# Row sums of a 67 MB tensor: splitting the first load by 64 bytes per partition in place of one row

## The chip, the cores and the metric

The kernel runs on one core of one Trainium2 chip. The metric is device time in microseconds (us) of that core, as the median of several executions. Spans and event times come from one profiled execution, counted from its first instruction; a span is some 1.8 us shorter than the time of the same execution.

## The reference

The input has 32 x 512 rows of 1024 float32 values, and each row is summed.

```python
def setup_inputs():
    return {"x": np.random.randn(32, 512, 1024).astype(np.float32)}

def reference(x):
    return np.sum(x, axis=-1).astype(np.float32)
```

So 67.1 MB are read and 65 KB are written, and there is one addition per value.

## The kernel before

Partition p of a block reads `n` whole rows that follow one another in memory. Three buffers of 16 rows per partition (8 MB each) take turns; a load of buffer k+3 waits for the reduction of buffer k. The first buffer alone is filled by two loads. The first `EARLY` instructions of the issuing engine (SP), which are these two loads, are moved ahead of the start barrier.

```python
BLOCKS = (112, 16)
G = 16
EARLY = 2
...
    xpool = ctx.enter_context(tc.tile_pool(name="x", bufs=3))
...
        while c < whole:
            m = min(G, whole - c)
            xt = xpool.tile([P, G * D], F32, tag="xt", name="xt")
            parts = (0, 1, m) if done + c == 0 else (0, m)
            for i, k in zip(parts, parts[1:]):
                nc.sync.dma_start(
                    out=xt[:, i * D : k * D], in_=x_b[:, (c + i) * D : (c + k) * D]
                )
            a = ACT_ROWS if done + c + m == full else 0
            rows_dve(xt, res, 0, m - a, c)
            rows_act(xt, res, m - a, a, c + m - a)
            c += m
# ... the last 16 rows are loaded in five smaller pieces and summed on VectorE and ScalarE ...
    loads = [i for i in code if i.engine == sp][:EARLY]
# ... these loads are taken out of the body and put ahead of the start barrier ...
```

## Time and profile before

| | before |
|---|---|
| time, median of 3 (range) | 162.22 us (162.12 to 162.32) |
| span of the profiled execution | 160.6 us |
| full-width reduction, and the load it waits for | 17.22 us, every 19.35 us |
| one packet of 65536 bytes on one DMA engine | 2418 ns |
| last data landed | 157.8 us |

These are lines of the profile page of the kernel before: the span; VectorE's (DVE) busy time; the busy share of the DMA engines in 40 slices, in tenths; the chain of work that ended last; the costliest group; and the larger of the first two loads, with its size and the time from issue to landing.

```profile
span 160.6 us, 119 instructions
...
DVE 121.5 (76%) x16; ACT 17.2 (11%) x31; POOL 0.2 (0%) x4
...
DMA  9988996996996996996996996996996996998991
...
DMA 75%; DVE 23%; SPq 0%; issue 0%; DVEq 0%
...
L43 DVE TENSOR_REDUCE res<-xt 128x16 f32<-128x16384 f32 (+3 forms) x9 | 119.8, 13309 | 36.5 <-DMA xt<-in_x_dram 36.5
...
xt<-in_x_dram SPq DMA_DIRECT2D x1, 7680.0 KB, 21.5
...
```

DVE is busy for three quarters of the span, yet it isn't the limit, as its timeline shows. The columns are start, duration (both us), engine (in these views ACT is ScalarE and POOL is GpSimd), line, operation, operands, and in brackets the idle time before it with what ended that.

```profile
...
22.00 17.22 DVE L43 TENSOR_REDUCE res<-xt 128x16 f32<-128x16384 f32 x1 [22.00 <-DMA xt<-in_x_dram]
...
60.63 17.22 DVE L43 TENSOR_REDUCE res<-xt 128x16 f32<-128x16384 f32 x1 [2.13 <-DMA xt<-in_x_dram]
...
118.67 17.22 DVE L43 TENSOR_REDUCE res<-xt 128x16 f32<-128x16384 f32 x1 [2.13 <-DMA xt<-in_x_dram]
138.03 9.75 DVE L43 TENSOR_REDUCE res<-xt 128x9 f32<-128x9216 f32 x1 [2.13 <-DMA xt<-in_x_dram]
...
158.21 0.08 DVE L59 DVE_READ_ACCUMULATOR2_ANT res<- 128x1 f32 x1
```

The full-width reductions take 17.22 us, and from the third on each one starts only after a wait of 2.13 us for a DMA. Consecutive ones start 19.35 us apart (118.67 less 60.63, over three). The loads set the pace.

The records of single DMA packets, which the page sums up, give the pace of a load. One packet is one partition's contiguous run, and each of the 16 DMA engines takes eight of them per load, one after the other (the records don't name the engine; I read this from starts that follow ends). A packet of 65536 bytes takes 2418 ns and one of 4096 bytes 159 ns, so the rate is (65536 - 4096) / (2418 - 159) = 27.2 bytes per ns with some 8 ns per packet on top. Sixteen engines make 435 GB/s of it. The Trainium skill, "DMA: Bandwidth & Descriptors", section Specifications, gives 435 GB/s as the fabric ceiling; this trace agrees. Later loads are issued about 20 us before an engine gets to them (one was issued at 39.24 us and its first packet started at 59.50 us), so from its first packet on no engine is short of work.

That makes the start worth a look. The following lines are stretches of the first 6 us of the kernel before. After the stretch and its length come the busy times of the compute engines, then the clock, the busy share of the DMA engines, and GB/s.

```profile
...
core 0: us, DVE busy (x) ACT busy (x) POOL busy (x), PEclk, DMA share, GB/s
0.00:0.90 0.90, 0.00 (x0) 0.00 (x0) 0.20 (x4) 1.00 0.00 0
0.90:1.45 0.55, 0.00 (x0) 0.00 (x0) 0.00 (x0) 1.00 1.15 156
1.45:2.60 1.15, 0.00 (x0) 0.00 (x0) 0.00 (x0) 1.00 0.75 267
2.60:3.45 0.85, 0.00 (x0) 0.00 (x0) 0.00 (x0) 1.00 3.05 1311
...
4.90:5.90 1.00, 0.00 (x0) 0.00 (x0) 0.00 (x0) 1.00 2.27 983
...
```

In this view a packet is booked whole in the stretch in which it starts, so a share far above 1 means long packets starting. From 2.60 to 3.45 us, 1311 GB/s over 0.85 us are 1114 KB: sixteen packets of 61440 bytes and the last 32 of the row load. From 0.90 to 2.60 us only the row load runs. At full rate its eight packets per engine need 8 x 159 ns = 1.27 us, but they last from about 1.1 to 3.0 us, because the first ones of each engine took up to 828 ns. I call this loss, packet times above the full-rate time, the *slow start*: summed and divided by 16 it comes to 0.55 us per engine here, all within the row load. The big packets behind it had none (2267 to 2274 ns).

The row load's landing, by the list of DMA issues (size and time from issue to landing; its other line is the rest of the first buffer):

```profile
...
xt<-in_x_dram SPq DMA_DIRECT2D x1, 7680.0 KB, 21.5
...
xt<-in_x_dram SPq DMA_DIRECT2D x1, 512.0 KB, 3.8
...
```

### The profile page before, as it was taken

Reading aid. Unit: us, or ns where it says so; the run is one execution under the profiler, and the core shown is the slowest. Engines: PE = TensorE matmul, PEld = TensorE weight load, DVE = VectorE, ACT = ScalarE, POOL = GpSimd, SP = SyncE. Lnnn points to the kernel's source line nnn. Section 1 sums busy time; section 2 is a strip of 40 time slices with the busy share of each in tenths; the row PEclk is TensorE's granted clock in tenths of the full one; section 3 lists DMA queues with packets and bytes.
Section 4 is the critical chain, followed back from the end, with each engine's and each line's share of the span. In section 5 each row is a group of like instructions: output and inputs, shape, how many; then the busy total and the mean of one; then the engine's idle time right before and its main releaser. Section 6 shows DMA issues by size and latency. Waiting matters only on the chain.

```text
span 160.6 us, 119 instructions
## 1 busy us (share of the span) xinstructions
DVE 121.5 (76%) x16; ACT 17.2 (11%) x31; POOL 0.2 (0%) x4
## 2 busy tenths in 40 slices
DVE  0000059997799959999499994999949998697884
ACT  0000000000000000000000000000000000695892
POOL 0000000000000000000000000000000000000000
DMA  9988996996996996996996996996996996998991
GB/s 375 490 367 367 490 522 277 506 522 277 506 522 261 522 522 261 522 522 261 522 506 277 522 506 277 522 506 277 522 506 277 522 490 294 441 431 364 436 390 44
DMA packets 2160, 67.18 MB, mean 418 GB/s; under 512 B 496, under 2 KB 624, under 8 KB 880
## 3 DMA queue, kind: packets, MB, share of 16 engines
q1 hardware_dynamic: 2016, 67.12, 97.2%
q10 hardware_dynamic: 144, 0.06, 0.1%
HBM read 67.11 MB, written 0.07 MB: 418 GB/s over the span
## 4 chain that ended last, share of the span: by engine, by line
DMA 75%; DVE 23%; SPq 0%; issue 0%; DVEq 0%
DMA xt<-in_x_dram 75%; DVE res L43 21%; DVE pairs L59 1%; SPq L95 0%; DVE seen L112 0%; DVE part L59 0%; DVE res L59 0%; DVEq L120 0%
## 5 line engine op out<-in xcount | busy, mean ns | idle before, releaser
L43 DVE TENSOR_REDUCE res<-xt 128x16 f32<-128x16384 f32 (+3 forms) x9 | 119.8, 13309 | 36.5 <-DMA xt<-in_x_dram 36.5
L51 ACT ACT_TABLE_LOAD x1 | 1.3, 1283 | 138.1 <-DMA xt<-in_x_dram 138.1
L51 ACT ACTIVATE xt<-xt 128x1024 f32<-128x1024 f32 x15 | 15.6, 1044 | 2.4 <-DMA xt<-in_x_dram 2.3
L51 ACT ACTIVATION_READ_ACCUMULATOR xt<-xt 128x1 f32 x15 | 2.8, 187 | 0.0
L59 DVE CUSTOM_DVE_ANT_0 pairs<-xt 128x512 f32<-128x512 f32 (+1 forms) x2 | 1.1, 567 | 0.2 <-DMA xt<-in_x_dram 0.2
L59 DVE CUSTOM_DVE_ANT_0 pairs<-xt,part 128x240 f32<-128x240 f32 x1 | 0.5, 468 | 0.0
L112 DVE COPY seen<-part 128x1 f32<-128x1 f32 x1 | 0.2, 153 | 0.0
L59 DVE DVE_READ_ACCUMULATOR2_ANT res<- 128x1 f32 x2 | 0.2, 83 | 0.0
L157 POOL MEMSET const-uint8-127<- 128x1 uint8 x1 | 0.1, 102 | 0.0
L157 POOL MEMSET const-bfloat16-1.0<- 128x1 bf16 x1 | 0.1, 101 | 0.0
L157 POOL MEMSET const-float32-0.0<- 128x1 f32 x1 | 0.1, 99 | 0.2 <-issue 0.2
L157 POOL MEMSET const-float32-1.0<- 128x1 f32 x1 | 0.1, 99 | 0.0
L59 DVE DVE_READ_ACCUMULATOR2_ANT part<- 128x1 f32 x1 | 0.1, 83 | 0.0
## 6 DMA issues: line engine op xcount, KB each, us to landing
xt<-in_x_dram SPq DMA_DIRECT2D x1, 7680.0 KB, 21.5
xt<-in_x_dram SPq DMA_DIRECT2D x1, 4608.0 KB, 32.5
xt<-in_x_dram SPq DMA_DIRECT2D x1, 2048.0 KB, 37.1
xt<-in_x_dram SPq DMA_DIRECT2D x1, 1024.0 KB, 39.1
xt<-in_x_dram SPq DMA_DIRECT2D x1, 512.0 KB, 3.8
xt<-in_x_dram SPq DMA_DIRECT2D x1, 272.0 KB, 39.3
xt<-in_x_dram SPq DMA_DIRECT2D x1, 240.0 KB, 39.4
xt<-in_x_dram SPq DMA_DIRECT2D x6, 40.8
```

What stands on the lines that cost most here:

```text
L43: nc.vector.tensor_reduce(out=res[:, c : c + n], in_=xt[:, j * D : (j + n) * D].rearrange("p (j d) -> p j d", d=D), axis=X, op=ADD,)
L51: nc.scalar.activation(out=v, in_=v, func=COPY, accum_out=acc)
L59: nc.vector.tensor_tensor_reduce(out=pairs[:, 0 : h - a], in0=xt[:, a:h], in1=xt[:, h:b], scale=1.0, scalar=first, op0=ADD, op1=ADD, accum ...
L112: nc.vector.tensor_copy(out=seen, in_=part)
L157: nc = _bacc.Bacc("TRN2", target_bir_lowering=False, num_devices=1)
```

## The change

The intent: the first load need only be there to get the engines going, so make it as small as can be (64 bytes per partition, 8 KB in all) and leave everything else to one bulk load of 65472 bytes per partition, hoping that the tiny packets take the slow first accesses on themselves.

```diff
-            parts = (0, 1, m) if done + c == 0 else (0, m)
+            parts = (0, 16, m * D) if done + c == 0 else (0, m * D)
             for i, k in zip(parts, parts[1:]):
                 nc.sync.dma_start(
-                    out=xt[:, i * D : k * D], in_=x_b[:, (c + i) * D : (c + k) * D]
+                    out=xt[:, i:k], in_=x_b[:, c * D + i : c * D + k]
                 )
```

The order of instructions on each engine stays the same; only the shapes of the first two loads on SP differ.

## The prediction

> **What bounds the kernel now.** The input DMA. In the chain of waits the DMA of xt holds 75% of the 160.6 us span and DVE 23%, but DVE isn't the limit: each 128x16384 reduction takes 17.22 us and then waits 2.13 us for its load (timeline); loads complete every 19.35 us. In the DMA records each of 16 engines takes its packets back to back, 2418 ns for 65536 bytes, 159 ns for 4096: 27.2 bytes/ns plus about 8 ns a packet. Sixteen give 434 GB/s; the Trainium skill, "DMA: Bandwidth & Descriptors", Specifications, gives a fabric ceiling of 435 GB/s, and the trace agrees. Engines run without idle time from the first packet (1.00 us) to the last data (157.47 us); later loads are issued some 20 us before their turn. So only the start of each engine's stream and the tail can move the time, and the diff leaves the tail alone.
>
> **The start of before.** Issue of the row load begins at 0.00 us (0.376 us long), of the fifteen rows at 0.43 us. First packets start at 1.00 to 1.27 us. Eight packets of 4096 bytes per engine need 1.27 us at full rate but end at 2.70 to 3.42 us: the first two or so take 240 to 830 ns in place of 159. The 61440-byte packets follow without a gap. Counting back at full rate (19.41 us) from the end of the first buffer (20.82 to 21.54 us), each engine behaves as if it had started, without loss, at 1.41 to 2.13 us. The last engine carries its 0.7 us lag to the end and decides the time.
>
> **What the change does.** In the comparison of instruction orders only the first two SP loads differ; counts of loads and packets, semaphores, waits, DVE and ACT work stay. Each engine gets eight packets of 64 bytes and eight of 65472. Full-rate time is unchanged, by an estimate from the rates above: 8 x (11 + 2415) = 19.41 us. (64-byte packets of the final store took up to 11 ns; 1920-byte packets starting at an odd multiple of 128 bytes took the 79 ns that the rate predicts, so I expect no loss from the offset.) Gained: the small packets may absorb the slow first accesses. Lost: they run out at once, and the bulk can't flow before its own descriptors arrive, 0.43 us after the first load's, at 1.43 to 1.70 us, plus what it still meets of the first-read latency (0.1 to 0.65 us above full rate). Effective start: 1.5 to 2.3 us against 1.4 to 2.1. I expect a wash with a slight loss, +0.1 us, all on the critical path, since the stream has no slack. The same section of the skill puts line rate at 512 bytes and up; 128 tiny packets are too few to matter.
>
> **Prediction.** 162.3 us, 161.95 to 162.75 with 8 in 10. Faster by over 2%: 0.005; within 2%: 0.985; slower: 0.01.
>
> **What would show it.** The small load landing at 2 to 2.5 us instead of 3.8; first 65472-byte packets starting at 1.5 to 2.2 us, 2415 ns each; first buffer ending at 20.8 to 21.7 us; then every event shifted by one constant, with unchanged 2.13 us DVE waits and unchanged tail.
>
> **What would make it wrong.** The 64-byte offset lowering the bulk rate (5% would cost about 1 us, still within 2%); small packets served one after another at a full read latency each (8 x 0.24 us: +0.3 us or more); or the slow start being due to the volume moved in it, so that small packets even out the engines and the last one gains 0.3 us.

## The result, and the profile after

| | before | after |
|---|---|---|
| time, median of 6 runs each (range) | 162.27 us (162.12 to 162.49) | 162.81 us (162.76 to 162.90) |
| ratio after / before, 95% interval | | 1.0034 (1.0021 to 1.0047) |
| span of the profiled execution | 160.6 us | 161.0 us |

The change is 0.5 us slower. By a margin of 2% that is "the same", but the difference is clear of the noise, and it lies outside the range that I gave.

The same lines of the profile page of the kernel after:

```profile
span 161.0 us, 119 instructions
...
DVE 121.5 (75%) x16; ACT 17.2 (11%) x31; POOL 0.2 (0%) x4
...
DMA  7999999999999999999999999999989989998991
...
DMA 75%; DVE 22%; SPq 0%; issue 0%; DVEq 0%
...
L43 DVE TENSOR_REDUCE res<-xt 128x16 f32<-128x16384 f32 (+3 forms) x9 | 119.8, 13309 | 36.9 <-DMA xt<-in_x_dram 36.9
...
xt<-in_x_dram SPq DMA_DIRECT2D x1, 8184.0 KB, 22.0
...
```

The work is the same; the first slice of the DMA row fell from 9 tenths to 7. That digit does not measure the loss: in this row too a packet counts whole where it starts, and the first slice of one_load, an experiment below that runs in the time of before, is 7 as well. DVE's timeline of the kernel after:

```profile
...
22.52 17.22 DVE L43 TENSOR_REDUCE res<-xt 128x16 f32<-128x16384 f32 x1 [22.52 <-DMA xt<-in_x_dram]
...
61.13 17.22 DVE L43 TENSOR_REDUCE res<-xt 128x16 f32<-128x16384 f32 x1 [2.13 <-DMA xt<-in_x_dram]
...
119.17 17.22 DVE L43 TENSOR_REDUCE res<-xt 128x16 f32<-128x16384 f32 x1 [2.13 <-DMA xt<-in_x_dram]
138.53 9.76 DVE L43 TENSOR_REDUCE res<-xt 128x9 f32<-128x9216 f32 x1 [2.13 <-DMA xt<-in_x_dram]
...
158.60 0.08 DVE L59 DVE_READ_ACCUMULATOR2_ANT res<- 128x1 f32 x1
```

The first reduction starts 0.52 us later, and the later full-width ones stay 0.50 us late with the same waits of 2.13 us: a constant shift, as expected from a stream without slack. In the tail 0.1 us of it is gone in this pair of profiles (158.60 against 158.21). The two profiled executions took 162.43 and 162.82 us, 0.39 apart, while the medians are 0.54 apart: the profiled one of the kernel before was a little slow, so nothing is to be read into that 0.1.

The start of the kernel after, in the same stretches:

```profile
...
core 0: us, DVE busy (x) ACT busy (x) POOL busy (x), PEclk, DMA share, GB/s
0.00:0.90 0.90, 0.00 (x0) 0.00 (x0) 0.20 (x4) 1.00 0.00 0
0.90:1.45 0.55, 0.00 (x0) 0.00 (x0) 0.00 (x0) 1.00 0.16 15
1.45:2.60 1.15, 0.00 (x0) 0.00 (x0) 0.00 (x0) 1.00 2.70 911
2.60:3.45 0.85, 0.00 (x0) 0.00 (x0) 0.00 (x0) 1.00 0.00 0
...
4.00:4.90 0.90, 0.00 (x0) 0.00 (x0) 0.00 (x0) 1.00 2.19 946
4.90:5.90 1.00, 0.00 (x0) 0.00 (x0) 0.00 (x0) 1.00 0.45 196
...
```

The 1048 KB booked from 1.45 to 2.60 us (911 GB/s times 1.15 us) are exactly 16 packets of 65472 bytes: each engine's first bulk packet starts in this stretch, at 1.49 to 2.33 us by the packet records. The tiny packets before it had ended by 1.47 us, at 8 to 11 ns each: they show no slow start at all. And the second bulk packets start only from 4.58 us on, for the first ones took up to 3424 ns, not 2415. So the engines had next to nothing to do until the bulk came, and then the bulk had its slow start in full: 0.72 us per engine on average.

The list of DMA issues of the kernel after, for the two loads:

```profile
...
xt<-in_x_dram SPq DMA_DIRECT2D x1, 8184.0 KB, 22.0
...
xt<-in_x_dram SPq DMA_DIRECT2D x1, 8.0 KB, 1.8
...
```

The tiny load has landed 1.8 us after its issue, and nothing waits for it that early.

### The profile page after: what moved, and what is told of

Read it like the earlier page. It is cut to its first block, busy times and chain, and to the rows that moved or that the text cites. A ratio compares the mean times of both kernels' runs of the same rounds, so it can differ in the third digit from the quotient of the medians.

```text
span 161.0 us, 119 instructions
## 1 busy us (share of the span) xinstructions
DVE 121.5 (75%) x16; ACT 17.2 (11%) x31; POOL 0.2 (0%) x4
## 4 chain that ended last, share of the span: by engine, by line
DMA 75%; DVE 22%; SPq 0%; issue 0%; DVEq 0%
DMA xt<-in_x_dram 75%; DVE res L43 21%; DVE pairs L59 1%; SPq L95 0%; DVE seen L112 0%; DVE part L59 0%; DVE res L59 0%; DVEq L120 0%
```

## The experiments

Theory D: the first useful bytes come later by the interval between the issues of the two loads, 0.43 us, since the tiny load runs out before the bulk's packets can start. (0.43 us lie between the starts of the two issuing instructions. Between their ends it is 0.47 us, and that is the better measure: where its engines were free, a load's first packet started 0.60 to 0.66 us after the end of its issuing instruction, in every run.) The slow start is a cost of getting bulk bytes going, and a tiny load doesn't take it over. Rivals: the offset of 64 bytes or the odd size slows the bulk (O); tiny packets are costly by themselves (S); the slow start is a period after the launch that passes by itself (C, for cold; W is a variant, a warming by the row). Three more bear on what the slow start is: far addresses (P), the issue of further loads (G), or any start from rest (R).

Diffs are against the kernel after. Each kernel was timed in the same rounds as the kernel before, whose median was 162.32 us beside one_load, bulk_first, two_tiny and after_e1, and 162.22 us beside the others. All of these kernels gave correct results. The table collects the packet records; "bulk" means the packets of over 60000 bytes that fill the first buffer, slow starts are averages per engine, and the buffer's end is the end of its last packet. The packet columns are of one profiled execution each, which need not be the median one: that of one_load, at 162.59 us, was the slowest of five. The time of the profiled execution less its buffer's end is 140.67 to 140.98 us in all of these kernels but contig (141.35), so what the last engine loses at the start goes into the time whole.

```
                  first load    slow start  bulk issued  first bulk     slow start   buffer's   median us, and ratio to
run               per partition of it, us   at us        packets, mean  of bulk, us  end, us    before (same rounds)
before            4096 B        0.55        0.43         3.00           0.00         21.54      162.27
after             64 B          0.00        0.43         1.69           0.72         22.06      162.81  1.0034
one_load          none          -           0.00         1.13           0.78         21.76      162.36  1.0003
bulk_first        (64 B after)  -           0.00         1.19           0.69         21.42      162.35  1.0002
after_e1          64 B          0.00        0.77         2.00           0.63         22.35      163.06  1.0044
two_tiny          2 x 64 B      0.00        0.88         2.13           0.80         22.68      163.13  1.0052
b256              256 B         0.00        0.42         1.74           0.82         22.23      162.94  1.0040
kb1               1024 B        0.12        0.41         1.72           0.69         21.73      162.56  1.0024
kb2               2048 B        0.24        0.43         2.15           0.32         21.72      162.26  1.0003
before_e1         4096 B        0.52        0.77         2.97           0.05         21.58      162.45  1.0015
contig            none          -           0.00         1.18           0.62         21.37      162.42  1.0014
gated             none          -           0.00         1.26           0.66         21.68      162.43  1.0009
```

### One load for the first buffer (one_load)

```diff
-            parts = (0, 16, m * D) if done + c == 0 else (0, m * D)
+            parts = (0, m * D)
```

> The first buffer in one load of 128 x 65536 bytes, issued first. Theory D (the change costs the wait for the descriptors of the bulk; the slow start of about 0.6 us is paid by whatever carries the first real bytes): first bulk packets start at 1.0 to 1.3 us and take about 3.1 us, end of the first buffer 20.9 to 21.6 us, time 162.3 us, as before. Theory W (a first load of a whole row warms something up): the slow start grows, time 162.6 or more. Rivals O (the offset of 64 bytes costs) and S (tiny packets cost) also say 162.3.

Measured: 162.36 us, ratio 1.0003 (0.9990 to 1.0016). In the stretches of this kernel fifteen engines start their first big packet from 0.90 to 1.45 us (1787 GB/s over 0.55 us are 983 KB) and one just after, and the second packets start from 4.00 to 4.90 us, some 3.2 us later:

```profile
...
0.90:1.45 0.55, 0.00 (x0) 0.00 (x0) 0.00 (x0) 1.00 5.52 1787
1.45:2.60 1.15, 0.00 (x0) 0.00 (x0) 0.00 (x0) 1.00 0.14 57
...
4.00:4.90 0.90, 0.00 (x0) 0.00 (x0) 0.00 (x0) 1.00 2.69 1165
...
```

The row load of the kernel before thus bought nothing. W falls: with no row ahead of it the slow start was no worse in its effect on time. The slow start is here too, in the bulk.

### The same two loads in reversed order (bulk_first)

```diff
-            for i, k in zip(parts, parts[1:]):
+            for i, k in reversed(list(zip(parts, parts[1:]))):
```

> The two loads of the change in reversed order: 65472 bytes at offset 64 first, the 64 bytes after it. D: 162.3 us, the whole loss of 0.54 us is gone, though tiny packets and offset are still there; first 65472-byte packets start at 1.0 to 1.3 us. O or S: stays at 162.8.

Measured: 162.35 us, ratio 1.0002 (0.9989 to 1.0014). The stretches:

```profile
...
0.90:1.45 0.55, 0.00 (x0) 0.00 (x0) 0.00 (x0) 1.00 5.02 1667
1.45:2.60 1.15, 0.00 (x0) 0.00 (x0) 0.00 (x0) 1.00 0.30 114
...
4.00:4.90 0.90, 0.00 (x0) 0.00 (x0) 0.00 (x0) 1.00 2.68 1164
...
```

The same sizes, the same offset, the same tiny packets, and the whole loss is gone once the bulk is issued first. This clears O and S. The 64-byte packets, issued at 0.43 us, started only at 20.92 us, when the bulk packets of their engine were through. The Trainium skill, "DMA: Bandwidth & Descriptors", section Queues, rings and completion order, says that on each DMA engine descriptors are consumed in ring order; this run agrees. It is why the order of the two loads matters at all.

### Two tiny loads ahead of the bulk (two_tiny)

```diff
-EARLY = 2
+EARLY = 3
-            parts = (0, 16, m * D) if done + c == 0 else (0, m * D)
+            parts = (0, 16, 32, m * D) if done + c == 0 else (0, m * D)
```

> Two loads of 64 bytes before the bulk, all three issued early. D: the bulk is issued one issue interval (0.45 to 0.48 us) later than in the changed kernel, so 163.25 to 163.3 us, first bulk packets at about 1.95 us. S: about 0.5 more as well if the packets cost, but then bulk packets start late by more than the issue. O: 162.8.

Measured: 163.13 us, ratio 1.0052 (1.0039 to 1.0064). The bulk was issued 0.45 us later than in the kernel after, its first packets started 0.44 us later on average (2.13 against 1.69), and the time rose by 0.3 us in place of the 0.45 to 0.5 expected. With the width of the two intervals (0.2 us each way) that isn't clearly less than the delay. Second bulk packets now start after 4.90 us:

```profile
...
1.45:2.60 1.15, 0.00 (x0) 0.00 (x0) 0.00 (x0) 1.00 2.86 917
...
4.00:4.90 0.90, 0.00 (x0) 0.00 (x0) 0.00 (x0) 1.00 0.00 0
4.90:5.90 1.00, 0.00 (x0) 0.00 (x0) 0.00 (x0) 1.00 2.43 1047
...
```

### The bulk issued after the start barrier (after_e1)

```diff
-EARLY = 2
+EARLY = 1
```

> The changed kernel with only the 64-byte load issued early; the bulk is issued after the start barrier, at about 1.26 us instead of 0.43. D with a slow start that comes anew with each start of a bulk stream: +0.83 us over the changed kernel, 163.6 us, first bulk packets from 2.3 us still 0.6 to 0.9 us too long. If the slow start is a period after the launch that passes by itself: first bulk packets near 2.42 us long, time 162.9 to 163.1 us.

Measured: 163.06 us, ratio 1.0044 (1.0031 to 1.0056). My number for D missed, because I had taken the issue time from the kernel before: with only one load ahead of it the barrier was passed earlier, and the bulk was issued at 0.77 us, not 1.26. From 0.43 to 0.77 us are 0.34 us, and the time rose by 0.25. Measured at the end of the bulk's issuing instruction (0.855 us in the kernel after, 1.102 us here) the delay is 0.25 us too. The time alone fits what I wrote for C, but not the packets: thirteen of the sixteen first bulk packets took 2973 to 3434 ns, the slow start was 0.63 us per engine. So it did not pass by itself.

### A first load of 256 bytes (b256)

```diff
-            parts = (0, 16, m * D) if done + c == 0 else (0, m * D)
+            parts = (0, 64, m * D) if done + c == 0 else (0, m * D)
```

> The small load holds 256 bytes of each run, 2 KB per engine, 0.14 us at full rate (8 packets of about 18 ns). D: it is used up before the bulk arrives, as the 64-byte one was, so nearly the whole loss stays: 162.65 to 162.8 us. If only the 64 bytes are bad, or the slow start is paid by this load: 162.3.

Measured: 162.94 us, ratio 1.0040 (1.0027 to 1.0052), a little above what I expected. All small packets were through by 1.34 us, and the bulk's slow start was 0.82 us.

### A first load of 1024 bytes (kb1)

```diff
-            parts = (0, 16, m * D) if done + c == 0 else (0, m * D)
+            parts = (0, 256, m * D) if done + c == 0 else (0, m * D)
```

> The small load holds 1024 bytes of each run, 8 KB per engine. D: in the kernel before an engine had moved about 8 KB by 2.05 us, later than the descriptors of the bulk arrive (1.5 to 2.0 us), so no engine runs dry and the loss is gone: 162.3 us, within 0.15. If any first load smaller than a row costs: 162.6 or more.

Measured: 162.56 us, ratio 1.0024 (1.0012 to 1.0037). D's number missed. I had thought that 8 KB per engine last until 2.05 us, since they did as part of the row load. As small packets they had gone by 1.70 us, with little slow start of their own:

```profile
...
0.90:1.45 0.55, 0.00 (x0) 0.00 (x0) 0.00 (x0) 1.00 0.63 151
1.45:2.60 1.15, 0.00 (x0) 0.00 (x0) 0.00 (x0) 1.00 2.79 939
...
4.00:4.90 0.90, 0.00 (x0) 0.00 (x0) 0.00 (x0) 1.00 1.82 788
...
```

The 16 bulk packets begin in the same stretch as in the kernel after, and their slow start is nearly whole (0.69 us). Moving 8 KB per engine first fills most of the wait: by an estimate from the table the small packets are through at 1.13 + 8 x 0.046 + 0.12 = 1.62 us on average, 0.1 us before the bulk starts, where the 64-byte ones left 1.69 - (1.13 + 8 x 0.011) = 0.47 us idle. But it doesn't pay for the slow start, which is 0.12 + 0.69 = 0.81 us in the two loads together, against 0.78 in one_load. The waiting and the slow start add up, and that part of D stands; what fell is my idea of when the slow start is paid.

### A first load of 2048 bytes (kb2)

```diff
-            parts = (0, 16, m * D) if done + c == 0 else (0, m * D)
+            parts = (0, 512, m * D) if done + c == 0 else (0, m * D)
```

> The small load holds 2048 bytes of each run, 16 KB per engine (0.67 us at full rate). With 1024 bytes the small packets were through by 1.70 us and the bulk still began 0.5 us late and slow; with 4096 nothing was lost. Theory D with a slow start that belongs to bytes in bulk: the small load ends at about 2.1 to 2.4 us, after the bulk's descriptors are there, so 162.3 to 162.45 us. If each first load short of a row costs the same: 162.55 or more.

Measured: 162.26 us, ratio 1.0003 (0.9987 to 1.0019): the loss is gone. The small packets last to 2.34 us, and the slow start is shared: 0.24 us in them and 0.32 us in the bulk. With the row (4096 bytes) it lies wholly in the first load. That 2048 bytes are enough and 1024 are not rests on the timed runs alone, whose intervals overlap a little (0.9987 to 1.0019 and 1.0012 to 1.0037): the two profiled executions took 162.48 and 162.50 us, with the buffer's end at 21.72 and 21.73 us.

### The kernel before with its bulk issued after the barrier (before_e1)

```diff
-EARLY = 2
+EARLY = 1
```

> The kernel before with only the row load issued early: the bulk is issued at about 0.77 us, not 0.43. D: the row keeps the engines busy to 2.7 to 3.4 us, the descriptors of the bulk are there from about 1.7 to 2.5 us, so no change: 162.3 us; 61440-byte packets of 2267 ns without a slow start. If a later bulk issue costs by itself, as it did behind 64 bytes: 162.6.

(This diff alone is against the kernel before.) Measured: 162.45 us, ratio 1.0015 (0.9996 to 1.0035), with one run of six at 163.33 us that widens the interval. The bulk was issued at 0.77 us, as in after_e1, but behind a row it didn't matter: its first packets started at 2.75 to 3.21 us, straight after the row packets, and the buffer ended at 21.58 us. The timing alone doesn't settle it, with an interval that reaches from nothing to 0.6 us; the packet records do: no engine waited for its bulk, and the bulk's slow start was 0.05 us.

### The first buffer's data contiguous in memory (contig)

```diff
-BLOCKS = (112, 16)
+BLOCKS = (16, 96, 16)
-            parts = (0, 16, m * D) if done + c == 0 else (0, m * D)
+            parts = (0, m * D)
```

> One load for the first buffer, and the row blocks as 16, 96, 16 so that its 8 MB are contiguous in memory and not 128 runs at a distance of 448 KB. Theory P (the slow start of about 0.7 us comes from the many far addresses touched at once): first packets near 2418 ns, 161.7 us. Theory R (it is what starting an idle stream costs, wherever the data lies): first packets 3.0 to 3.6 us as in the run with one load, 162.3 us, the extra 8 KB store costing under 0.1.

Measured: 162.42 us, ratio 1.0014 (1.0001 to 1.0026). The first packets took 2651 to 3286 ns, a slow start of 0.62 us against 0.78 with one load of runs 448 KB apart. P falls as the main cause; a small share can't be excluded. The time is no test of it here: the first buffer ended at 21.37 us, 0.39 us before that of one_load, but the next reductions started up to 19.47 us apart, not about 19.35 as in one_load, and of the lead at the first reduction (0.39 us) 0.04 us was left at the fifth.

### No other loads issued meanwhile (gated)

```diff
-EARLY = 2
+EARLY = 1
+            if done + c == G:
+                nc.gpsimd.memset(xt[:, 0:4096], 0.0)
-            parts = (0, 16, m * D) if done + c == 0 else (0, m * D)
+            parts = (0, m * D)
```

> One load for the first buffer; the second load first waits for a fill of 128x4096 elements on GpSimd, some microseconds, so that no further loads are issued while the first packets run. Theory G (issuing the next loads slows the first packets): first packets near 2418 ns, 161.7 us. Theory R: first packets 3.0 to 3.6 us as before, 162.3 us, since the second load still comes long before the first is done.

Measured: 162.43 us, ratio 1.0009 (0.9996 to 1.0023). The second load was issued at 4.32 us, after every engine's first packet had been under way for over 2 us, and those first packets took 2453 to 3549 ns all the same. G falls.

### One buffer, so that every load starts from rest (one_buf)

```diff
-    xpool = ctx.enter_context(tc.tile_pool(name="x", bufs=3))
+    xpool = ctx.enter_context(tc.tile_pool(name="x", bufs=1))
-EARLY = 2
+EARLY = 1
-            parts = (0, 16, m * D) if done + c == 0 else (0, m * D)
+            parts = (0, m * D)
```

> One buffer, so that each of the seven big loads is issued only when the reduction before it is through and every stream starts from rest: a slow kernel on purpose, about 270 us. Theory R (a cost of every start from rest): the first packet of each engine in every one of these loads takes 3.0 to 3.6 us. Theory C (something that is cold only at launch): 3.0 to 3.6 us in the first load and near 2.42 us in the later ones.

Measured: 293.9 us in its single run (state unknown, which matters little for a look at packets). My 270 was too low: I had left out the last 16 rows, whose loads were issued only from 266.87 us on and took the span to 292.1 us. The stretches around the second load, which was issued at 39.21 us:

```profile
...
39.20:40.10 0.90, 0.00 (x0) 0.00 (x0) 0.00 (x0) 1.00 0.00 0
40.10:40.60 0.50, 0.00 (x0) 0.00 (x0) 0.00 (x0) 1.00 6.37 2097
40.60:43.00 2.40, 0.00 (x0) 0.00 (x0) 0.00 (x0) 1.00 0.00 0
43.00:44.20 1.20, 0.00 (x0) 0.00 (x0) 0.00 (x0) 1.00 2.02 874
44.20:45.30 1.10, 0.00 (x0) 0.00 (x0) 0.00 (x0) 1.00 0.00 0
45.30:46.70 1.40, 0.00 (x0) 0.00 (x0) 0.00 (x0) 1.00 1.73 749
...
```

2097 GB/s over 0.50 us, 874 over 1.20 and 749 over 1.40 are 1049 KB each time, 16 packets of 65536 bytes. The first 16 start about 40.3 us, the second 16 some 3.2 us later, the third 2.4 us after those. By the packet records the slow start of the seven loads was 0.76, 0.78, 0.86, 0.78, 0.74, 0.70 and 0.55 us per engine. So R holds and C falls: each start of the stream from rest pays it on average, at launch or 235 us later.

## Why the prediction was wrong

**Right.** The DMA bound and the missing slack: the whole shift of the first buffer went through every later load (0.52, then 0.50 us). The count of instructions and waits stayed, and the packets behind the first kept their rate (2415 to 2422 ns for 106 of 112, the longest 2622), with no loss from the offset of 64 bytes. I also had the sign and the mechanism of the loss: "Lost: they run out at once, and the bulk can't flow before its own descriptors arrive, 0.43 us after the first load's". Issue first and the loss goes (bulk_first); issue later still and it grows (after_e1, two_tiny).

**Wrong.** The failed step is the term set against that loss: "Gained: the small packets may absorb the slow first accesses." They absorbed nothing. Their packets took 8 to 11 ns, and the bulk behind them lost 0.72 us per engine, as much as a bulk with nothing ahead of it (0.78 in one_load). I had counted on the gain to cancel all but 0.1 of the 0.43 us; with the gain at zero the loss stands whole, and 0.54 us was measured. In the sum of the prediction this is the term "what it still meets of the first-read latency (0.1 to 0.65 us above full rate)": it measured 0.72 us on average, and up to 1.01 us in a single first packet. The other term was a little short as well: the bulk was to flow "at 1.43 to 1.70 us", and its first packets started at 1.49 to 2.33 us, 1.69 on average. The table above has the sum: mean start of the bulk plus its slow start was 1.69 + 0.72 = 2.41 us after, and 1.13 + 0.78 = 1.91 us in one_load, which runs in the time of before: 0.5 us apart, all of it from the later start.

So the "effective start" came out wrong: "1.5 to 2.3 us against 1.4 to 2.1" should have been 2.08 to 2.65 (the ends of the engines' work on the first buffer, 21.49 to 22.06 us, less 19.41). The last engine decides, and it went from 2.13 to 2.65 us. Two observations of the prediction fell with it: "2415 ns each" for the first bulk packets (they took 2422 to 3424) and "first buffer ending at 20.8 to 21.7 us" (21.49 to 22.06). The small load landed at 1.8 us, earlier than "2 to 2.5", which fits with its having met no slow accesses. The starting times of the first bulk packets (1.5 to 2.2 us predicted, 1.49 to 2.33 found) were nearly right.

Of my listed ways to be wrong none was it. The rate did not fall; the small packets were not served at a latency each; they did not even out the engines.

What stays open is what the slow start is. The runs show when it is paid: at each start of the stream from rest, by packets of 1024 bytes and up (little by those of 1024), and not by 64 or 256 bytes per packet. It isn't a fixed price of each engine's own start: in the kernels and loads with a slow start of the bulk, thirteen first packets began over 0.75 us after the first one of their load, and they lost 0 to 0.34 us, where the averages are 0.32 to 0.86. In the kernel after, the engine that came last (at 2.33 us) took 2422 ns. This suggests that it belongs to the stretch in which the engines start together. The runs rule out the launch (one_buf), the issue of further loads (gated) and mostly the distance of the addresses (contig). They don't show the mechanism. All loads here were issued by SP one after another; whether a bulk load issued at the same time by another engine would be spared the wait was not tried.

No kernel here beats that of before. One load for the first buffer equals it (1.0003) and is the simplest; a row first, or half a row (kb2), is as good.

## What to carry to other kernels

When DMA is the bound and its stream never runs dry, the time moves with the first moment at which the last engine has bulk work: put the bulk first, and don't let a small load precede it in the same queue unless it holds enough bytes to bridge the interval to the next issue (here 2048 bytes per partition did, while 1024 still cost 0.3 us by the timed runs). Don't expect a tiny load to pay a start-up cost for a large one; look at the packets of the tiny one, and if they show no such cost they haven't paid it. A row-sized first load that looks tuned may do nothing, so try without it before tuning its size.

## What the Trainium skill lacked or had wrong

- "DMA: Bandwidth & Descriptors" has no slow start of a load stream from rest. Here a load of 65536 bytes per partition lost 0.55 to 0.86 us per engine on its first packets, at every one of seven starts (one_buf); loads of 64 or 256 bytes per partition showed none, and a load of 4096 bytes held all of it (0.55 us).
- The same page, section Issuing engines are not separate DMA queues, calls the issue time of a DMA "usually small relative to the DMA itself". That is so for a load of 20 us, but when the load ahead in the queue holds 8 KB in all, one issue interval of 0.43 us (0.47 from end to end) was most of the whole effect of 0.54 us.
- The same page, section Latency and other measured facts, gives about 0.6 us to the first byte for a DMA issued from SP. The traces agree only if one counts from the end of the issuing instruction: it began at 0.00 us and took 0.38, and the first packet started at 0.99 us in the kernel after. Counted so, it was 0.60 to 0.66 us in every run here. From the start of the issue it is 1.0 us, and the mean over the engines is 1.1 (one_load); the page doesn't say which is meant.
- The same page, section Specifications, puts line rate at 512 bytes and up. Below that the traces agree: packets of 64 bytes took 8 to 11 ns and packets of 256 bytes 15 to 18, at most 17 bytes per ns, where the full rate is 27.2. But above 512 bytes the rate still climbs: 22 bytes per ns at 1024 (46 ns), 24 at 2048 (84 ns), 26 at 4096 (159 ns).
